# Regrouping the attention part of a decoder block: all projections of q and k first, one stretch each for turning, probabilities and values, and the unseen corners of the scores set by VectorE

## The chip, the cores and the metric

The kernel runs on one core of one Trainium2 chip. The time is device time in microseconds (us) of one execution; the reported time is the median of several runs. Engines are named TensorE (PE, and PEld for its weight loads), VectorE (DVE), ScalarE (ACT), GpSimd (POOL) and SyncE (SP, which issues the large DMAs).

## The reference

One decoder block on 256 tokens with a model width of 1024, all in float32. Two attention branches of eight heads of width 64 run side by side on the same normalised input, are gated and added; then comes a gated feed-forward part with a short convolution. With 256 tokens the block-sparse branch ("MoBA", block of 256) has a single block, so it is plain causal attention; the other branch ("FoX") adds a forgetting bias to the scores.

```python
h = rms_norm(x, attn_norm_g)
proj = h @ w_in          # qa, ka, va, qb, kb, vb (512 each), f_logit (8), g_logit (2 x 1024)
qa, ka = partial_rope(rms_norm(qa, ...)), partial_rope(rms_norm(ka, ...))
o_a = causal_softmax(qa @ ka.T / 8) @ va
qb, kb = rms_norm(qb, ...), rms_norm(kb, ...)
c = cumsum(log_sigmoid(f_logit + b_forget))
o_b = causal_softmax(qb @ kb.T / 8 + c[t] - c[s]) @ vb
gates = sigmoid(g_logit + b_gate)
merged = gates[0] * (o_a @ w_branch_moba) + gates[1] * (o_b @ w_branch_fox)
x = x + merged @ w_out
u, g = split(rms_norm(x, ffn_norm_g) @ w_ffn_up)
x = x + (silu(causal_conv3(g)) * u) @ w_ffn_down
```

## The kernel before, in words

Every large product is made from three matmuls of a shorter float32 form (`F32R`): each weight and each activation is split in a high and a low part, and high times high, high times low and low times high are added. Weights come from memory in chunks of 128 x 2048 (1 MB), in the order of the list `chunks`, by DMAs on SP's queue into three buffers (`raw`, `RB`). Each half chunk (128 x 1024) is split once: ScalarE casts it to `whi` (L136) and VectorE subtracts to get `wlo` (L137). There are six buffers of each (`HB`), and `use` asks for the split five halves ahead (`AHEAD`). A half chunk then feeds 24 matmuls of 256 columns (`twin`, L511 to L513) or 12 of 512 (`project`, L291).

TensorE's instructions run in the order in which the program writes them (`manual_schedule`). The order of the other engines is worked out by the compiler's planner, from readiness and from priorities; `soon()` raises the priority of what stands in it, and `after(i, j)` puts instruction i behind j on the same engine.

PSUM has eight banks. `bank()` takes one of them for every result that TensorE makes: a projection takes two, a gate one, the scores of a branch six, `turn` six, `turn_qk` two, the values of a branch two. A bank comes free when its readers are done.

The attention part consists of these pieces. `project_qk` projects q and k of the MoBA branch while x arrives; `project(2)` and `project(5)` make V of the two branches, `project(3)` and `project(4)` q and k of FoX. `finish_qk` normalises q or k (and turns by the rotary angles for MoBA) on ScalarE and VectorE. `turn_qk` (L341) transposes q or k by TensorE in 16 small products, and ScalarE copies the results to `qT` and `kT` (L346). `scores` (L434) multiplies q and k; because of the causal mask only some of each 128 x 128 or 128 x 256 area is computed, in pieces of 64 rows, and the corners that no product fills get something finite by small bf16 products of ones (L437). `softmax` takes the row maxima and masks by VectorE (L448), exponentials by ScalarE (L451), and scales by VectorE (L453, L456). `turn` (L467) transposes the probabilities in 48 small products per branch; ScalarE copies them out (L471). `values` (L483) multiplies them with V; ScalarE and VectorE split the result into `oh` and `ol` (L497, L498). The forgetting bias is made by `forget_a` (L362, products with the forget weights), `forget_b` (L372), `forget_chain` (small functions, a running sum by VectorE, L388, and two DMAs on POOL's queue that spread it over the partitions, L391 and L393) and `forget_bias` (five VectorE operations of 128 x 1024, L408 to L414). Eight `gate(c)` are products of two half chunks each; VectorE reads the result (L520) and the sigmoids (L524) follow later.

Before, TensorE goes through them thus: q and k of MoBA; project(2); project(3); forget_a and two turns; the first half of project(4), with forget_b within; scores(0); the rest of project(4); project(5); gate(0); two turns and turn(0); gate(1); values(0) and scores(1); gate(2) to gate(6); turn(1); gate(7); values(1); then the branch products (L609 to L611), the output product and the feed-forward part, which do not change.

Of the kernel before, what the change touches and what calls it, by code (L numbers as in the profile page):

```python
# [8 lines left out]
F32 = mybir.dt.float32  # L9
# [8 lines left out]
P = 128  # L18
# [26 lines left out]
def decoder_block(ctx, tc, a, out):  # L45
# [35 lines left out]

    chunks = [("qkv", m, h) for m in range(4) for h in range(2)]
    chunks += [("wg", c) for c in range(KT)]
    chunks += [("wb", c) for c in range(4)]
# [17 lines left out]
    def load(upto):  # L102
        while state["next"] <= min(upto, len(units) - 1):
# [30 lines left out]
            for j in range(n):  # L134
                s = slice(j * w, (j + 1) * w)
                i = nc.scalar.activation(hi[:, s], raw[:, s], AF.Copy)  # L136
                d = nc.vector.tensor_tensor(lo[:, s], raw[:, s], hi[:, s].bitcast(F32), op=ALU.subtract)  # L137
                if (c, h) == (("qkv", 0, 1), 0):
                    after(i, rs_done[0])
                    after(d, rs_done[1])  # L140
                if (c, h) == (("qkv", 0, 0), 0):
                    first_lo.append(d)
                if c[0] == "head" and j == 0:
                    after(d, xlo)
# [91 lines left out]
    def norm1_sums():  # L236
        nc.scalar.activation(flat[:, 0], xss[:, 1], AF.Copy)
        low = nc.gpsimd.tensor_tensor(flat[:, 1], xss[:, 1], flat[:, 0].bitcast(F32), op=ALU.subtract)
        for i in casts:
            after(i, low)  # L240
        ssp = bank()[:, 0:S]
        for i in range(2):
            nc.tensor.matmul(ssp, first_ones, flat[:, i], start=(i == 0), stop=(i == 1))
        return ssp
# [48 lines left out]
    def finish_v(pt, m):  # L293
        c = slice(m * W4, (m + 1) * W4)
        nc.scalar.activation(V[:, 0, c], pt[0], AF.Copy, scale=rs[:, 0:1])
        for r, q in (halves, halves[::-1]):
            nc.scalar.activation(V[r, 1, c], pt[1][q], AF.Copy, scale=rs[q, 1:2])

    def finish_qk(br, pts):
        n = len(pts)  # L300
# [10 lines left out]
        for m, (isk, pt) in enumerate(pts):  # L311
            qn = T([P, NT, NH, HD], "qn", 2)
            qns.append(qn)
            for t in range(NT):
                nc.vector.tensor_tensor(qn[:, t], pt[t].rearrange("p (h d) -> p h d", h=NH),
                                        f[:, m, t, :, None].to_broadcast([P, NH, HD]), op=ALU.mult)
            if br == 0:
                rc, rsn = rope[isk]
                p1 = T([P, NT, NH, 16], "p1", 1)
                p2 = T([P, NT, NH, 16], "p2", 1)  # L320
                x16 = qn[:, :, :, 0:16]
                nc.vector.tensor_tensor(p1, x16, rc[:, :, None, :].to_broadcast([P, NT, NH, 16]), op=ALU.mult)
                nc.vector.tensor_tensor(p2, x16, rsn[:, :, None, :].to_broadcast([P, NT, NH, 16]), op=ALU.mult)
                nc.vector.tensor_tensor(qn[:, :, :, 0:8], p1[:, :, :, 0:8], p2[:, :, :, 8:16], op=ALU.add)
                nc.vector.tensor_tensor(qn[:, :, :, 8:16], p1[:, :, :, 8:16], p2[:, :, :, 0:8], op=ALU.add)
        return qns


    qT = T16(4, "qT", F32)
    kT = T16(4, "kT", F32)  # L330
    halves = (slice(0, HD), slice(HD, P))

    def turn_qk(qn, br, isk):
# [3 lines left out]
        for t in range(NT):  # L337
            for b in range(4):
                for h, r in enumerate(halves):
                    src = qn[r, t, 2 * b:2 * b + 2].rearrange("p h d -> p (h d)")  # L340
                    nc.tensor.transpose(tp[h][:, (4 * t + b) * HD:(4 * t + b + 1) * HD], src, ident[r, r])  # L341
        dst = (kT if isk else qT).rearrange("p b (m c) -> p m b c", m=4)
        places = (slice(2, 0, -1), slice(3, None, -3)) if isk else (slice(0, 4, 2), slice(1, 4, 2))
# [22 lines left out]
    def row(i):  # L366
        return gates[:NH, i // 2, i % 2]

# [47 lines left out]

    oh = T16(KT, "oh")
    ol = T16(KT, "ol")
    probs = {}
    last_exp = []  # L420

    def scores(br):
# [5 lines left out]
        for n, pair in enumerate(range(4)):  # L428
            for t in range(NT):
                for c, q in enumerate(QUARTERS[t]):  # L430
                    seen, unseen = (slice(0, (q + 1) * HD), slice((q + 1) * HD, P)) if t == 0 else (slice((3 - q) * HD, S), slice(0, (3 - q) * HD))
                    keys = slice(seen.start + (1 - t) * P, seen.stop + (1 - t) * P)
                    for j, r in enumerate(halves):
                        nc.tensor.matmul(piece(n, t, j)[halves[c], seen], qT[r, pair, q * HD:(q + 1) * HD], kT[r, pair, keys], start=True, stop=True)  # L434
                    if q % 2 == 0:
                        for j, r in enumerate(halves):
                            nc.tensor.matmul(piece(n, t, j)[halves[c], unseen], warm[r, 0:HD], warm[r, 0:HD], start=True, stop=True)  # L437
        return [[[piece(n, t, j) for t in range(NT)] for j in range(2)] for n in range(4)]

    def softmax(br, pair, sps):  # L440
        s = T([P, 2, 384], "s", 4)
        nm = T([P, 2, 2], "nm", 4)
        l = T([P, 2, 2], "l", 4)
        for j in range(2):
            h = 2 * pair + j
            sp = sps[j]
            for i, c in enumerate((slice(0, 128), slice(128, 384))):
                nc.vector.tensor_tensor_reduce(s[:, j, c], sp[i], mask3[:, c] if br == 0 else bias[:, h, c],  # L448
                                               scale=1.0, scalar=3e38, op0=ALU.add, op1=ALU.min, accum_out=nm[:, j, i:i + 1])
            for i, c in enumerate((slice(0, 128), slice(128, 384))):  # L450
                last_exp[:] = [nc.scalar.activation(s[:, j, c], s[:, j, c], AF.Exp, scale=-1.0, bias=nm[:, j, i:i + 1], accum_out=l[:, j, i:i + 1])]  # L451
# [8 lines left out]
    def turn(br):  # L460
        pT = T([P, 4, 2, 384], "pT")
        tps = [banks() for _ in range(3)]
# [11 lines left out]

    def values(br):
        ops = banks()
        o4 = [o.rearrange("p (h b t) -> p h b t", h=2, b=4) for o in ops]

        def product(o, r, k, b, c, pair, j, start, stop):
            vc = br * W4 + (2 * pair + j) * HD  # L480
# [4 lines left out]
        one, two, both, full = slice(0, 1), slice(1, 2), slice(0, 2), slice(0, P)  # L485
        for i, k, b, c in ((0, 0, 0, two), (1, 0, 2, both), (1, 1, 1, two)):
            for pair in range(4):
                for j, m in enumerate(halves):
                    product(o4[i][m, c, pair], full, k, b, c, pair, j, b != 1 and pair == 0, False)
        for pair in range(4):  # L490
            for j, m in enumerate(halves):
                product(o4[0][m, 0, pair], halves[0], 0, 0, one, pair, j, False, pair == 3)
                product(o4[1][m, 0, pair], halves[1], 1, 1, one, pair, j, False, pair == 3)
        b = slice(4 * br, 4 * br + 4)
        for i in range(2):
            h, l = (v[:, b, i * P:(i + 1) * P].rearrange("p b (h t) -> p h b t", h=2) for v in (oh, ol))
            nc.scalar.activation(h, o4[i], AF.Copy)  # L497
            nc.vector.tensor_tensor(l, o4[i], h.bitcast(F32), op=ALU.subtract)  # L498


# [15 lines left out]

    def gate(c):
        gp = bank()
        twin("wg", c, gp, xh, xl)
        return nc.vector.tensor_tensor(gates[:, c], gp.rearrange("p (b t) -> p b t", b=2), rsB[:, None, :].to_broadcast([P, 2, S]), op=ALU.mult)  # L520
# [12 lines left out]

    pq, pk, pv = banks(), banks(), banks()
    for k in range(KT):
# [7 lines left out]
    with soon():  # L543
        qn, kn = finish_qk(0, ((0, pq), (1, pk)))
    project(2, pv, 0)
    project(2, pv, 1)
    finish_v(pv, 0)
    pq, pk = banks(), banks()
    project(3, pq, 0)
    project(3, pq, 1)  # L550
    with soon():
        forget_a()
    turn_qk(qn, 0, 0)
    turn_qk(kn, 0, 1)
    with soon():
        qn, = finish_qk(1, ((0, pq),))
    def between():
        with soon():
            forget_b()
    project(4, pk, 0, between)  # L560
    with soon():
        sps = scores(0)
        for pair in range(2):
            done = softmax(0, pair, sps[pair])
    forget_chain(done)
    project(4, pk, 1)
    with soon():
        kn, = finish_qk(1, ((1, pk),))
    for pair in range(2, 4):
        done = softmax(0, pair, sps[pair])  # L570
    pv = banks()
    project(5, pv, 0)
    project(5, pv, 1)
    finish_v(pv, 1)
    first = gate(0)
    with soon():
        forget_bias(first)
    turn_qk(qn, 1, 0)
    turn_qk(kn, 1, 1)
    turn(0)  # L580
    gate(1)
    values(0)
    for pair, sp in enumerate(scores(1)):
        softmax(1, pair, sp)
    gate(2)
    gate(3)
    gate(4)
    gate(5)
    gate(6)
    turn(1)  # L590
    gate(7)
    values(1)
    sig = [gate_sigmoid(c) for c in range(KT)]
    tables = [nc.scalar.preload_act_table_set("natural_log_exp_and_others")]
    for i in sig:
        after(tables[0], i)
# [202 lines left out]
```

## Time and profile before

| | us |
|---|---|
| runs before (3): median, lowest, highest | 362.5, 362.5, 362.65 |
| the profiled execution: its own time | 362.39 |
| the profiled execution: span from the first to the last instruction | 360.6 |

The profile is a record of one execution. Its page gives, for each engine, the time it was busy and the share of the span; the chain that ended last, followed back from the last instruction; and the costliest groups of instructions, with source line, tiles, shapes, count, busy time and the mean of one in ns. A timeline lists an engine's instructions in order of time: start, duration, engine, line, operation, output tile <- inputs, shape and count; in brackets stands how long the engine was idle before it and what ended that. Matmuls overlap, so that the distance between two starts, not the duration shown, is what one costs. A table of waits says which engine waited for what, for how long in all, how often, and how long at most. The granted clock of TensorE was 0.998 over the span.

### The profile page before, as it was taken

How to read it: one execution, taken by the hardware profiler on the slowest of the kernel's cores; microseconds unless marked ns; L12 is line 12 of the kernel's file. 1: busy time of each engine (PE TensorE's matmuls, PEld its weight loads, DVE VectorE, ACT ScalarE, POOL GpSimd, SP SyncE). 2: the span in 40 equal slices, each digit the busy share in tenths (PEclk: the TensorE clock that was granted, in tenths of full speed). 3: DMA queues.
4: the chain of work that ended last, by engine and by line, in shares of the span. 5: the costliest groups of instructions: out<-in, count | busy, mean ns of one | idle time of the engine just before them, and what ended most of it. 6: DMA issues, size and time to landing. Idle time of an engine off the chain costs nothing.

```text
span 360.6 us, 7612 instructions
## 1 busy us (share of the span) xinstructions
PE 355.4 (99%) x3151; PEld 337.5 (94%) x3151; DVE 274.3 (76%) x471; ACT 218.3 (61%) x363; POOL 28.1 (8%) x43
## 2 busy tenths in 40 slices
PE   9999999999999999999999999999999999999995
PEld 4888878899999999999999999999999999999994
DVE  4899699999887547885969776868677776768643
ACT  5859667888697774545877654655464554555420
POOL 2542002300010000000530000000000000000000
PEclk9999999999999999999999999999999999999999
DMA  7987665373606644456364564464564464563003
GB/s 275 400 318 244 238 233 183 126 257 141 234 10 235 231 170 150 159 219 201 151 223 171 193 234 162 189 234 153 199 232 164 190 234 145 205 220 132 3 0 116
DMA packets 12130, 68.28 MB, mean 189 GB/s; under 512 B 1688, under 2 KB 2848, under 8 KB 4672
## 3 DMA queue, kind: packets, MB, share of 16 engines
q1 hardware_dynamic: 11664, 66.62, 51.3%
q0 software_dynamic: 288, 1.19, 1.0%
q8 instruction: 24, 0.39, 0.4%
q14 instruction: 10, 0.08, 0.1%
q10 hardware_dynamic: 144, 0.00, 0.0%
HBM read 66.75 MB, written 1.06 MB: 188 GB/s over the span
## 4 chain that ended last, share of the span: by engine, by line
PE 99%; DVE 0%; issue 0%
PE bank L511 15%; PE bank L512 15%; PE bank L513 15%; PE bank L291 12%; PE bank L277 6%; PE bank L712 6%; PE bank L713 6%; PE bank L711 6%; PE bank L609 2%; PE bank L611 2%; PE bank L637 2%; PE bank L610 2%; PE bank L636 2%; PE bank L635 2%; PE bank L483 1%; PE bank L434 1%
## 5 line engine op out<-in xcount | busy, mean ns | idle before, releaser
L137 DVE TENSOR_TENSOR wlo<-raw,whi 128x1024 fp32r<-128x1024 f32 x120 | 147.0, 1229 | 52.6 <-ACT whi L136 52.2
L136 ACT ACTIVATE whi<-raw 128x1024 fp32r<-128x1024 f32 x120 | 126.3, 1058 | 75.5 <-PE bank L512 44.6
L513 PE MATMUL bank<-oh,wlo 128*128 128x256 f32 x352 | 96.8, 275 | 0.0
L511 PE MATMUL bank<-oh,whi 128*128 128x256 f32 x352 | 96.8, 275 | 0.0
L512 PE MATMUL bank<-ol,whi 128*128 128x256 f32 x352 | 96.8, 275 | 0.0
L511 PEld LDWEIGHTS bank<-oh,whi 128*128 128x128 f32 x352 | 66.1, 188 | 0.0
L513 PEld LDWEIGHTS bank<-oh,wlo 128*128 128x128 f32 x352 | 66.1, 188 | 0.0
L512 PEld LDWEIGHTS bank<-ol,whi 128*128 128x128 f32 x352 | 66.1, 188 | 0.0
L511 PE MATMUL bank<-xh,whi 128*128 128x256 f32 x128 | 35.6, 278 | 0.0
L513 PE MATMUL bank<-xh,wlo 128*128 128x256 f32 x128 | 35.2, 275 | 0.0
L512 PE MATMUL bank<-xl,whi 128*128 128x256 f32 x128 | 35.2, 275 | 0.0
L511 PEld LDWEIGHTS bank<-xh,whi 128*128 128x128 f32 x128 | 24.0, 188 | 0.4 <-DVE nm L448 0.2
L512 PEld LDWEIGHTS bank<-xl,whi 128*128 128x128 f32 x128 | 24.0, 188 | 0.0
L513 PEld LDWEIGHTS bank<-xh,wlo 128*128 128x128 f32 x128 | 24.0, 188 | 0.0
L291 PE MATMUL bank<-whi,xh 128*128 128x512 f32 x64 | 21.2, 392 | 0.0
L291 PE MATMUL bank<-whi,xl 128*128 128x512 f32 x64 | 21.0, 388 | 0.0
L291 PE MATMUL bank<-wlo,xh 128*128 128x512 f32 x64 | 21.0, 388 | 0.0
L678 DVE TENSOR_TENSOR sq<-bank,rs 128x512 f32<-128x512 f32 x22 | 15.1, 692 | 6.6 <-PE bank L513 6.5
L609 PE MATMUL bank<-oh,whi 128*128 128x256 f32 x64 | 17.7, 277 | 0.0
L611 PE MATMUL bank<-oh,wlo 128*128 128x256 f32 x64 | 17.6, 275 | 0.0
L610 PE MATMUL bank<-ol,whi 128*128 128x256 f32 x64 | 17.6, 275 | 0.0
L635 PE MATMUL bank<-xh,whi 128*128 128x256 f32 x64 | 17.6, 275 | 0.0
(180 smaller groups left out, 748.5 us busy)
## 6 DMA issues: line engine op xcount, KB each, us to landing
raw<-in_wu SPq DMA_DIRECT2D x22, 1024.0 KB, 4.8
raw<-in_wd SPq DMA_DIRECT2D x11, 1024.0 KB, 4.8
raw<-in_qkv SPq DMA_DIRECT2D x8, 1024.0 KB, 5.3
raw<-in_wg SPq DMA_DIRECT2D x8, 1024.0 KB, 4.8
raw<-in_wb SPq DMA_DIRECT2D x4, 1024.0 KB, 4.8
raw<-in_wo SPq DMA_DIRECT2D x4, 1024.0 KB, 4.8
raw<-in_head SPq DMA_DIRECT2D x6, 512.0 KB, 6.6
gates<-cd POOLq DMA_DIRECT2D x1, 1024.0 KB, 5.3
```

Of the source, the lines that this page charges most:

```text
L136: i = nc.scalar.activation(hi[:, s], raw[:, s], AF.Copy)
L137: d = nc.vector.tensor_tensor(lo[:, s], raw[:, s], hi[:, s].bitcast(F32), op=ALU.subtract)
L277: nc.tensor.matmul(pt[t], lhs[:, k, t * P:(t + 1) * P], rhs, start=(k == 0 and i == 0), stop=(k == KT - 1 and i == 2))
L291: nc.tensor.matmul(pt[t], lhs[:, k, t * P:(t + 1) * P], rhs[:, c], start=(k == 0 and i == 0), stop=(k == KT - 1 and i == 2))
L511: nc.tensor.matmul(o, wh[:, w], mh[:, k], start=(k == 0 and i == 0), stop=False)
L512: nc.tensor.matmul(o, wh[:, w], ml[:, k], start=False, stop=False)
L513: nc.tensor.matmul(o, wl[:, w], mh[:, k], start=False, stop=(k == KT - 1 and i == 1))
L609: nc.tensor.matmul(o, wh[:, w], oh[:, 4 * br + k], start=(k == 0), stop=False)
L610: nc.tensor.matmul(o, wh[:, w], ol[:, 4 * br + k], start=False, stop=False)
L611: nc.tensor.matmul(o, wl[:, w], oh[:, 4 * br + k], start=False, stop=(k == 3))
L635: nc.tensor.matmul(o, wh[:, w], mh[:, k], start=(k == 0 and i == 0), stop=False)
L711: nc.tensor.matmul(o, wh[:, w], ah, start=(p == 0 and h == 0 and c == 0), stop=False)
```

## The change

The order of the pieces on TensorE becomes: q and k of MoBA; project(3); project(4); gate(0); gate(1); four turns and forget_a; gate(2) with forget_b within; scores(0); project(2); gate(3); scores(1); project(5); gate(4); gate(5); turn(0) and turn(1); gate(6); values of both branches; gate(7). The list of chunks follows that order. The corners of the scores are set to zero by VectorE: ten memsets on 64 partitions for each branch, eight corners of 64 columns for each half of the heads, instead of 16 bf16 products. In each branch the first reductions of a softmax are put behind VectorE's reading of the gate before it. Because both branches are now alive together, q and k of FoX and its probabilities get homes in tiles that are free at that time (`oh`, `ol`, `qn`, `bias`), and the small rows of the forget chain move to the second half of `gates`. The sum for the first norm goes to the bank of the warm-up matmuls.

```diff
-    chunks = [("qkv", m, h) for m in range(4) for h in range(2)]
-    chunks += [("wg", c) for c in range(KT)]
+    chunks = []
+    for m in (1, 2, "wg0", "wg1", "wg2", 0, "wg3", 3, "wg4", "wg5", "wg6", "wg7"):
+        chunks += [("wg", int(m[2:]))] if isinstance(m, str) else [("qkv", m, h) for h in range(2)]
...
-        ssp = bank()[:, 0:S]
+        ssp = wp[:, 0:S]
...
     def row(i):
-        return gates[:NH, i // 2, i % 2]
+        return gates[:NH, 4 + i // 2, i % 2]
...
                     for j, r in enumerate(halves):
-                        nc.tensor.matmul(piece(n, t, j)[halves[c], seen], qT[r, pair, q * HD:(q + 1) * HD], kT[r, pair, keys], start=True, stop=True)
-                    if q % 2 == 0:
-                        for j, r in enumerate(halves):
-                            nc.tensor.matmul(piece(n, t, j)[halves[c], unseen], warm[r, 0:HD], warm[r, 0:HD], start=True, stop=True)
+                        nc.tensor.matmul(piece(n, t, j)[halves[c], seen], qTs[br][r, pair, q * HD:(q + 1) * HD], kTs[br][r, pair, keys], start=True, stop=True)
+        for b, c, o in ((0, 0, slice(64, 512, 384)), (0, 1, slice(128, 129, 1)), (1, 1, slice(0, 512, 256)), (2, 0, slice(64, 256, 128)), (2, 1, slice(256, 257, 1))):
+            for j in range(2):
+                starts = range(o.start, o.stop, o.step)
+                u = sps[b][j][halves[c]].rearrange("p (g c) -> p g c", c=HD)[:, o.start // HD:starts[-1] // HD + 1:max(1, o.step // HD)]
+                nc.vector.memset(u, 0.0)
...
-    def softmax(br, pair, sps):
+    def softmax(br, pair, sps, done):
...
-                nc.vector.tensor_tensor_reduce(s[:, j, c], sp[i], mask3[:, c] if br == 0 else bias[:, h, c],
+                first = nc.vector.tensor_tensor_reduce(s[:, j, c], sp[i], mask3[:, c] if br == 0 else bias[:, h, c],
                                                scale=1.0, scalar=3e38, op0=ALU.add, op1=ALU.min, accum_out=nm[:, j, i:i + 1])
+                after(first, done)
...
+    for isk in range(2):
+        pt = banks()
+        project(3 + isk, pt, 0)
+        project(3 + isk, pt, 1)
+        with soon():
+            qkn += finish_qk(1, ((isk, pt),))
+    gate(0)
+    gate(1)
+    for i, qn in enumerate(qkn):
+        turn_qk(qn, i // 2, i % 2)
+    with soon():
+        forget_a()
...
+    read = gate(2, between)
+    with soon():
+        for pair, sp in enumerate(scores(0)):
+            scaled = softmax(0, pair, sp, read)
+            if pair == 1:
+                done = scaled
+    forget_chain(done)
+    pv = banks()
     project(2, pv, 0)
     project(2, pv, 1)
     finish_v(pv, 0)
+    read = gate(3)
     with soon():
+        forget_bias(read)
     with soon():
+        for pair, sp in enumerate(scores(1)):
+            softmax(1, pair, sp, read)
     pv = banks()
     project(5, pv, 0)
     project(5, pv, 1)
     finish_v(pv, 1)
     gate(4)
     gate(5)
+    turn(0)
+    turn(1)
     gate(6)
+    oh, ol, copied = values()
     gate(7)
```

In the new `values()` all products over whole rows of both branches come first, then those over half rows, branch by branch, each followed by its copies to `oh` and `ol`.

More of the change, by code (lines that the diff above doesn't have):

```diff
@@ L137, in load @@
                 d = nc.vector.tensor_tensor(lo[:, s], raw[:, s], hi[:, s].bitcast(F32), op=ALU.subtract)
-                if (c, h) == (("qkv", 0, 1), 0):
+                if (c, h) == (("qkv", 1, 1), 0):
                     after(i, rs_done[0])
                     after(d, rs_done[1])
-                if (c, h) == (("qkv", 0, 0), 0):
+                if (c, h) == (("qkv", 1, 0), 0):
                     first_lo.append(d)
@@ L297, in finish_v @@
             nc.scalar.activation(V[r, 1, c], pt[1][q], AF.Copy, scale=rs[q, 1:2])
+    qn1 = T16(KT, "ol", F32)
     def finish_qk(br, pts):
@@ L311, in finish_qk @@
         for m, (isk, pt) in enumerate(pts):
-            qn = T([P, NT, NH, HD], "qn", 2)
+            if br == 0:
+                qn = T([P, NT, NH, HD], "qn", 2)
+            else:
+                qn = qn1[:, 4 * isk:4 * isk + 4].rearrange("p k t -> p (k t)").rearrange("p (t h d) -> p t h d", t=NT, h=NH)
             qns.append(qn)
@@ L326, in finish_qk @@
         return qns
-    qT = T16(4, "qT", F32)
-    kT = T16(4, "kT", F32)
+    qk1 = T16(KT, "oh", F32)
+    qTs = T16(4, "qT", F32), qk1[:, 0:4]
+    kTs = T16(4, "kT", F32), qk1[:, 4:8]
     halves = (slice(0, HD), slice(HD, P))
@@ L341, in turn_qk @@
                     nc.tensor.transpose(tp[h][:, (4 * t + b) * HD:(4 * t + b + 1) * HD], src, ident[r, r])
-        dst = (kT if isk else qT).rearrange("p b (m c) -> p m b c", m=4)
+        dst = (kTs if isk else qTs)[br].rearrange("p b (m c) -> p m b c", m=4)
         places = (slice(2, 0, -1), slice(3, None, -3)) if isk else (slice(0, 4, 2), slice(1, 4, 2))
@@ L414, in forget_bias @@
                 nc.vector.tensor_tensor(dst, dst, mask3[:, None, j * P:(j + 1) * P].to_broadcast([P, NH, P]), op=ALU.add)
-    oh = T16(KT, "oh")
-    ol = T16(KT, "ol")
     probs = {}
+    homes = []
     last_exp = []
@@ L430, in scores @@
                 for c, q in enumerate(QUARTERS[t]):
-                    seen, unseen = (slice(0, (q + 1) * HD), slice((q + 1) * HD, P)) if t == 0 else (slice((3 - q) * HD, S), slice(0, (3 - q) * HD))
+                    seen = slice(0, (q + 1) * HD) if t == 0 else slice((3 - q) * HD, S)
                     keys = slice(seen.start + (1 - t) * P, seen.stop + (1 - t) * P)
                     for j, r in enumerate(halves):
-                        nc.tensor.matmul(piece(n, t, j)[halves[c], seen], qT[r, pair, q * HD:(q + 1) * HD], kT[r, pair, keys], start=True, stop=True)
-                    if q % 2 == 0:
-                        for j, r in enumerate(halves):
-                            nc.tensor.matmul(piece(n, t, j)[halves[c], unseen], warm[r, 0:HD], warm[r, 0:HD], start=True, stop=True)
-        return [[[piece(n, t, j) for t in range(NT)] for j in range(2)] for n in range(4)]
-    def softmax(br, pair, sps):
-        s = T([P, 2, 384], "s", 4)
+                        nc.tensor.matmul(piece(n, t, j)[halves[c], seen], qTs[br][r, pair, q * HD:(q + 1) * HD], kTs[br][r, pair, keys], start=True, stop=True)
[4 more added lines that the diff above has]
+                nc.vector.memset(u, 0.0)
+        return [[[piece(n, t, j) for t in range(NT)] for j in range(2)] for n in range(4)]
+    def softmax(br, pair, sps, done):
+        if br == 0:
+            s = T([P, 2, 384], "s", 4)
+        else:
+            if not homes:
+                two = T([P, KT * S + 64], "ol")
+                homes.extend(two[:, i * 768:(i + 1) * 768] for i in range(2))
+                homes.extend(T([P, 1024], "qn", 2)[:, 0:768] for i in range(2))
+            s = homes[pair].rearrange("p (j c) -> p j c", j=2)
         nm = T([P, 2, 2], "nm", 4)
@@ L460, in turn @@
     def turn(br):
-        pT = T([P, 4, 2, 384], "pT")
+        pT = T([P, 4, 2, 384], ("pT", "bias")[br])
         tps = [banks() for _ in range(3)]
@@ L473, in turn, with values, product @@
             probs[br, pair] = pT[:, pair]
[L475 to L479, printed above, removed]
+    def values():
+        oh, ol = T16(KT, "oh"), T16(KT, "ol")
+        ops = [banks() for br in range(2)]
+        o4s = [[o.rearrange("p (h b t) -> p h b t", h=2, b=4) for o in ops[br]] for br in range(2)]
+        def product(o, r, k, b, c, br, pair, j, start, stop):
             vc = br * W4 + (2 * pair + j) * HD
@@ L485, in values @@
         one, two, both, full = slice(0, 1), slice(1, 2), slice(0, 2), slice(0, P)
-        for i, k, b, c in ((0, 0, 0, two), (1, 0, 2, both), (1, 1, 1, two)):
+        for br, o4 in enumerate(o4s):
+            for i, k, b, c in ((0, 0, 0, two), (1, 0, 2, both), (1, 1, 1, two)):
+                for pair in range(4):
+                    for j, m in enumerate(halves):
+                        product(o4[i][m, c, pair], full, k, b, c, br, pair, j, b != 1 and pair == 0, False)
+        for br, o4 in enumerate(o4s):
             for pair in range(4):
                 for j, m in enumerate(halves):
[L489 to L498, printed above, removed]
+                    product(o4[0][m, 0, pair], halves[0], 0, 0, one, br, pair, j, False, pair == 3)
+                    product(o4[1][m, 0, pair], halves[1], 1, 1, one, br, pair, j, False, pair == 3)
+            b = slice(4 * br, 4 * br + 4)
+            for i in range(2):
+                h, l = (v[:, b, i * P:(i + 1) * P].rearrange("p b (h t) -> p h b t", h=2) for v in (oh, ol))
+                copied = nc.scalar.activation(h, o4[i], AF.Copy)
+                nc.vector.tensor_tensor(l, o4[i], h.bitcast(F32), op=ALU.subtract)
+        return oh, ol, copied
     def twin(kind, c, dst, mh, ml, late=False, between=None):
@@ L515, in twin, with gate @@
                     between()
-    def gate(c):
+    def gate(c, between=None):
         gp = bank()
-        twin("wg", c, gp, xh, xl)
+        twin("wg", c, gp, xh, xl, between=between)
         return nc.vector.tensor_tensor(gates[:, c], gp.rearrange("p (b t) -> p b t", b=2), rsB[:, None, :].to_broadcast([P, 2, S]), op=ALU.mult)
@@ L532, in banks @@
         return [bank() for _ in range(NT)]
-    pq, pk, pv = banks(), banks(), banks()
+    pq, pk = banks(), banks()
     for k in range(KT):
@@ L543, in decoder_block, with between @@
     with soon():
-        qn, kn = finish_qk(0, ((0, pq), (1, pk)))
+        qkn = finish_qk(0, ((0, pq), (1, pk)))
+    for isk in range(2):
[10 more added lines that the diff above has]
+        forget_a()
+    def between():
+        with soon():
+            forget_b()
+    read = gate(2, between)
+    with soon():
+        for pair, sp in enumerate(scores(0)):
[4 more added lines that the diff above has]
+    pv = banks()
     project(2, pv, 0)
@@ L547, in decoder_block @@
     finish_v(pv, 0)
-    pq, pk = banks(), banks()
-    project(3, pq, 0)
-    project(3, pq, 1)
+    read = gate(3)
     with soon():
-        forget_a()
-    turn_qk(qn, 0, 0)
-    turn_qk(kn, 0, 1)
+        forget_bias(read)
     with soon():
[L556 to L570, printed above, removed]
+        for pair, sp in enumerate(scores(1)):
+            softmax(1, pair, sp, read)
     pv = banks()
@@ L574, in decoder_block @@
     finish_v(pv, 1)
[L575 to L586, printed above, removed]
     gate(4)
     gate(5)
+    turn(0)
+    turn(1)
     gate(6)
-    turn(1)
+    oh, ol, copied = values()
     gate(7)
-    values(1)
     sig = [gate_sigmoid(c) for c in range(KT)]
     tables = [nc.scalar.preload_act_table_set("natural_log_exp_and_others")]
-    for i in sig:
+    for i in sig + [copied]:
         after(tables[0], i)
```

## The prediction

> **What bounds the kernel now.** I read the busy line and the chain of the page first, then TensorE's and its weight load's waits, then TensorE's timeline around each place where the change moves something, and then VectorE's and ScalarE's timelines there.
>
> ```profile
> span 360.6 us, 7612 instructions
> PE 355.4 (99%) x3151; PEld 337.5 (94%) x3151; DVE 274.3 (76%) x471; ACT 218.3 (61%) x363; POOL 28.1 (8%) x43
> PE 99%; DVE 0%; issue 0%
> PEld bank L277 <- DVE wlo L137: 0.9, 3, 0.3
> ```
>
> The chain of waits lies on TensorE for 99%, and the weight loads waited 0.9 us for the splits, all of it in the start (L277). So the change can gain only what shortens TensorE's own stream, and it loses whatever makes TensorE wait. About 0.2% (0.7 us) is what can be told from no change here.
>
> The stream of weight matmuls keeps a fixed step, 0.113 us for 256 columns (122.35 to 122.46 below), so 24 of them, a half chunk, take 2.72 us. It is broken by six stretches of small matmuls: forget_a with two turns; scores(0); two turns with turn(0); values(0) with scores(1); turn(1); values(1). One of them, turn(1), and the two switches inside stretches:
>
> ```profile
> 122.35 0.28 PE L512 MATMUL bank<-xl,whi 128*128 128x256 f32 x1
> 122.46 0.28 PE L513 MATMUL bank<-xh,wlo 128*128 128x256 f32 x1
> 122.67 1.72 PE L467 MATMUL bank<-cst,s 64*128 64x64 f32 x48
> 124.31 0.39 PE L511 MATMUL bank<-xh,whi 128*128 128x256 f32 x1
> 124.54 0.28 PE L512 MATMUL bank<-xl,whi 128*128 128x256 f32 x1
> ...
> 131.63 0.34 PE L483 MATMUL bank<-pT,V 128*64 128x64 f32 x6
> 131.96 0.29 PE L483 MATMUL bank<-pT,V 64*64 64x64 f32 x4
> ...
> 49.06 1.07 PE L362 MATMUL bank<-xT,wfg 128*32 128x256 f32 x16
> 50.07 1.21 PE L341 MATMUL bank<-cst,qn 64*128 64x64 f32 x32
> 51.20 0.49 PE L291 MATMUL bank<-whi,xh 128*128 128x512 f32 x1
> ```
>
> The first stream matmul that turn(1) displaces was due at 122.57 and, counted back from 124.54, the stream is in step again from 124.43: 1.86 us. Its 24 pairs step by 0.061 us (1.46 us), so entering, draining and leaving cost 0.40 us a stretch. A switch of tile inside costs less: at 131.96 the next pair was due at about 131.86, and it restarts slowly, some 0.15 us in all.
>
> **The change part by part.**
>
> *One stretch fewer.* After: four turns with forget_a; scores(0); scores(1); turn(0) with turn(1); both values. Five for six: -0.40 us. Inside, values changes from whole to half rows once instead of twice, and turns and forget_a still meet once: two switches for three, -0.15 us. Projections and gates change places; each half is 2.72 us wherever it stands, and the chunks' list moves in step, each load the same 1024 KB on SP's queue, so nothing there.
>
> *Corners.* Each scores call makes 16 bf16 products of 64 columns (L437) that the memsets replace.
>
> ```profile
> 57.73 0.20 PE L437 MATMUL bank<-const-bfloat16-1.0 64*64 64x64 bf16 x2
> 57.76 0.30 PE L434 MATMUL bank<-kT,qT 64*64 64x128 f32 x6
> 57.88 0.20 PE L437 MATMUL bank<-const-bfloat16-1.0 64*64 64x64 bf16 x2
> 58.33 0.20 PE L437 MATMUL bank<-const-bfloat16-1.0 64*64 64x64 bf16 x2
> ```
>
> A pair of heads takes 0.60 us (57.73 to 58.33). On each half of the columns one corner sits in the row of products: 57.73 to 57.76 is 0.03 us, the lower bound. The other corner (57.88) stands in the way of the products issued behind it and can cost as much again, since all start in order. I take 0.055 us a pair, eight pairs: -0.44 us (bounds -0.22 to -0.50).
>
> *The wait in the turns.* All work shares eight PSUM banks; turns fill them and ScalarE empties them.
>
> ```profile
> 82.70 1.92 PE L467 MATMUL bank<-cst,s 64*128 64x64 f32 x48
> 83.91 0.71 PE L467 MATMUL bank<-cst,s 64*128 64x64 f32 x15
> 84.55 0.39 PE L511 MATMUL bank<-xh,whi 128*128 128x256 f32 x1
> 81.64 1.06 ACT L136 ACTIVATE whi<-raw 128x1024 fp32r<-128x1024 f32 x1 [1.66 <-PE bank L512]
> 82.61 1.25 ACT L346 ACTIVATE qT<-bank,gq 128x512 f32<-128x512 f32 x2
> 84.89 3.05 ACT L471 ACTIVATE pT<-bank 128x512 f32<-128x512 f32 x6
> 123.69 0.49 ACT L524 ACTIVATE gates<-gates,sm 128x256 f32<-128x256 f32 x1
> 124.08 3.01 ACT L471 ACTIVATE pT<-bank 128x512 f32<-128x512 f32 x6
> ```
>
> The stretch from 81.65 needs ten banks; the last two are waited for until ScalarE, busy with a cast until 82.61, has emptied two, at 83.86: turn(0) goes on at 83.91, and turn(0) here takes 1.85 us where turn(1) took 1.64. That wait goes: -0.19 us. But turn(0) with turn(1) needs twelve banks. From its start at T, a group of 16 transposes takes 0.49 us; the fifth group (T+2.0) needs two banks empty, the sixth (T+2.5) four. ScalarE takes the cast of the half whose buffer has just come free, T to T+1.0, then 0.50 us a bank (3.05 us for six): two at T+2.0, four at T+3.0. So the sixth waits: +0.49 us. If ScalarE begins at once there is no wait; with a gate's sigmoid between cast and copies, as at 123.69, it is 0.9. In the first stretch four turns fill exactly eight banks, gate(1)'s being read 0.7 us after T and needed at T+1.6; forget_a's is the first emptied: 0.
>
> *VectorE.* Its work is hidden as long as the splits stay ahead of TensorE.
>
> ```profile
> 81.76 0.69 DVE L520 TENSOR_TENSOR gates<-bank,rsB 128x512 f32<-128x512 f32 x1 [0.51 <-PE bank L513]
> 82.37 1.22 DVE L411 TENSOR_TENSOR bias<-gates,cc 128x1024 f32<-128x1024 f32 x1
> 88.04 2.35 DVE L137 TENSOR_TENSOR wlo<-raw,whi 128x1024 fp32r<-128x1024 f32 x2
> 94.78 0.28 DVE L448 CUSTOM_DVE_ANT_0 s<-bank,bias 128x128 f32<-128x128 f32 x1
> 97.00 0.18 DVE L453 RECIPROCAL r<-l 128x4 f32<-128x4 f32 x1 [0.27 <-ACT s L451]
> 101.91 1.22 DVE L137 TENSOR_TENSOR wlo<-raw,whi 128x1024 fp32r<-128x1024 f32 x1
> L456 DVE TENSOR_SCALAR s<-s,r 128x128 f32<-128x128 f32 x16 | 4.5, 281 | 0.0
> L448 DVE DVE_READ_ACCUMULATOR2_ANT nm<- 128x1 f32 x32 | 2.6, 83 | 0.0
> ```
>
> The 20 memsets (64 partitions, 64 or 128 elements) have no row. Between the smallest VectorE instruction (0.08 us) and a 128x128 one (0.28) I take 0.19: 1.9 us a branch (0.8 to 2.8). They stand ahead of the softmax, and all reductions behind them wait. The Trainium skill (VectorE: DVE Perf Modes, Zero memsets can be issued as uint32) gives a memset one cycle per element; with the 0.96 GHz of Trainium Kernel Development and Optimization (NeuronCore Architecture) that is an estimated 1.1 us a branch for its 1024 elements, without a fixed cost, and the count of the next paragraph would then end 0.8 us earlier, on time; no run so far shows a memset in PSUM.
>
> The tight place is after gate(3). Before, bias (82.37 to 88.04, 5.67 us) and softmax(1) (94.78) lay apart, with splits and 8 us of small matmuls between. Now they adjoin. Counting from the end of gate(3): evacuation until 0.7, bias until 6.4, memsets until 8.3, softmax(1) until its first split (7.13 us by 94.78 to 101.91) 15.4, that split 16.6. TensorE, with six buffers (HB), wants that half (gate(4)'s second, whose buffer came free at 0) after scores(1) (four pairs of 0.55 us and 0.40: 2.6) and five halves: 16.2. So in strict order it is 0.4 us late, and 1.6 us if one more split was owed when bias began. But its cast is done at 1.1, so it can go into any idle moment of VectorE, of the kind that stands before 97.00. The trace cannot tell: in that softmax no split was ready earlier. I take 0, bounds 0 and 2.5 (one split owed, memsets at 0.28). Elsewhere there is cover: softmax(0) after scores(0) has 16.3 us (six halves) until scores(1) wants its banks; the two later finish_qk stand 10.9 us apart and their results are wanted only at the turns.
>
> *The forget chain* starts later too.
>
> ```profile
> 60.02 0.28 DVE L448 CUSTOM_DVE_ANT_0 s<-bank,cst 128x128 f32<-128x128 f32 x1
> 68.76 0.58 POOL L393 DMA_DIRECT2D gates<-cd  x1
> gates<-cd POOLq DMA_DIRECT2D x1, 1024.0 KB, 5.3
> ```
>
> Its scan waits for the second pair's softmax, and the last of its DMAs is issued 8.7 us behind softmax(0)'s first reduction and lands 5.3 us later. After the end of gate(2) come scores(0) and the memsets (4 us), so it lands at 18; bias wants it after scores(0), project(2), gate(3) and an evacuation: 2.6 + 10.9 + 5.4 + 0.7 = 19.6. Hidden by 1.6 us; if late, VectorE stops in front of bias with splits queued behind it.
>
> *Rows, homes, banks, sigmoids.* Other buffers, the same instructions. values(1) stands a gate earlier than before, so its copies get 5.4 us more cover. 0.
>
> **Sum.** -0.40 -0.15 -0.44 -0.19 +0.49 = -0.69 us. The profiled execution took 362.39 us, 1.79 around its span of 360.6, which the change doesn't touch: 361.7. The median of the runs is 0.11 above it: 361.8.
>
> **The rivals.**
>
> *No wait in the turns.* ScalarE empties from T+0.6 on: against it, at 81.64 and at each gate's end it takes the cast. Then 361.8 - 0.5 = 361.3.
>
> *VectorE late after gate(3).* For it, the count above with no slack; against it, the ready split needs only one gap. 1.6 us: 363.4; it ends slower once it is over 1.4 us (from -0.69 to +0.7), and at its bound 2.5 us it is 364.3.
>
> *The change does little.* Corners at their lower bound (+0.22) and turns at 0.9 (+0.4): 362.4, no change.
>
> *The clock falls.* In the long transpose stretch the grant could drop, and the first half chunk behind it would take double: +2.72, 364.5. Against it, the clock stands at 1.00 through the transposes of before:
>
> ```profile
> 81.60:84.60 3.00, 3.00 (x83) 2.77 (x81) 2.84 (x3) 2.96 (x5) 0.00 (x0) 1.00 0.87 347
> ```
>
> The Trainium skill (TensorE: Matmul & The Clock Gate, Part 4) says that transposes don't count as work for the gate in the same way, and Part 1 puts the window at 3.4 us; the new stretch takes 3.8 us by the rows above (48 pairs of 0.061, 0.40 and 0.49). The trace shows no drop in 2.9 us, and no run before has more.
>
> **How the numbers follow.** Forecast 46% (361.4 to 362.2; 0.28 of it below 361.78, the 0.2% line, 0.18 above); no wait in the turns 12%, faster; little 11%, same; VectorE late 24% (0.11 same, 0.13 slower); clock 3% and a wait in the new order that I don't foresee 4%, slower. Faster 0.40, same 0.40, slower 0.20. The range reaches from 361.1 (0.2 us below the rival without a wait, since the price of a stretch is read off one of six) to 363.5 (VectorE late by 1.6 us), leaving out the rest.
>
> **What would show it.** Right: TensorE with five stretches, no L437 row, scores stretches shorter by about 0.2 us each, a gap of half a microsecond within L467's last group that ends when ScalarE has emptied the fourth bank, TensorE's sum of waits else unchanged. Wrong: TensorE or its weight loads waiting for wlo about 16 us after gate(3), or for banks in gate(4); or VectorE idle before bias, waiting for the DMA of cB; or a granted clock below 1.00 behind the turns.

## The result, and the profile after

| | us |
|---|---|
| before, 4 runs beside it | 362.57 (362.5 to 362.71) |
| after, 4 runs | 367.82 (367.15 to 368.02) |
| ratio, 95% interval | 1.0144 (1.0132 to 1.0156) |
| the profiled execution of after: own time, span | 367.73, 365.9 |

The changed kernel is 5.25 us slower. The forecast was 361.8 with a range to 363.5, so it failed in sign and in size. Times and ratios here leave out two disturbed executions, one of a1 (600.65 us, the only one of a1 with a trace) and one of a3 (727.45 us).

The first lines of the page of after, its busy line and its chain of waits:

```profile
span 365.9 us, 7562 instructions
PE 357.4 (98%) x3119; PEld 340.3 (93%) x3119; DVE 275.8 (75%) x491; ACT 218.1 (60%) x363; POOL 26.8 (7%) x43
PE 84%; ACT 7%; DVE 6%; issue 1%; ACTq 0%
```

Before, the chain lay on TensorE for 99%. Now 13% of it runs over ScalarE and VectorE: TensorE stood still somewhere for work of theirs. The table of waits between 110 and 123 us (engine, line, what it waited for, total us, times, longest) says where:

```profile
PEld bank L483 <- DVE gates L539: 3.0, 2, 2.7
PE bank L483 <- DVE gates L539: 2.6, 1, 2.6
PEld bank L483 <- ACT pT L487: 1.0, 3, 0.3
```

L483 is the transposing of the probabilities. It waited for banks: first for VectorE's reading of two gates (L539), then for ScalarE's copies (L487). No row names wlo, the wait that the prediction feared. TensorE's timeline there (start, duration, engine, line):

```profile
112.85 1.72 PE L483 MATMUL bank<-cst,s 64*128 64x64 f32 x48
114.70 0.27 PE L483 MATMUL bank<-cst,ol 64*128 64x64 f32 x1
118.89 0.46 PE L483 MATMUL bank<-cst,ol 64*128 64x64 f32 x7 [0.21 <-ACT pT L487]
119.13 1.84 PE L483 MATMUL bank<-cst,qn 64*128 64x64 f32 x24
...
120.90 0.58 PE L530 MATMUL bank<-xh,whi 128*128 128x256 f32 x1
121.28 0.41 PE L531 MATMUL bank<-xl,whi 128*128 128x256 f32 x1
```

turn(0) runs through in 1.5 us. turn(1) (tiles `ol` and `qn`) gets its first bank at 114.70, and its next product starts 2.87 us later. Between starts there are then 0.37, 0.48 and 0.48 us more, each ended by a copy. The stretch lasts 112.85 to 120.90, 8.05 us; without a wait it is 3.3 (d1 below: 3.51 with one wait of 0.25). Behind it the stream steps by 0.213 us instead of 0.113: the clock. Windows of the span (PE busy, PEld, DVE, ACT, POOL, granted clock, DMA share, GB/s):

```profile
112.60:116.00 3.40, 2.24 (x52) 1.84 (x51) 3.40 (x6) 3.39 (x5) 0.00 (x0) 1.00 0.84 296
116.00:119.40 3.40, 1.49 (x32) 1.22 (x32) 2.73 (x3) 3.40 (x8) 0.00 (x0) 1.00 0.76 263
119.50:122.80 3.30, 3.15 (x28) 2.85 (x26) 0.00 (x0) 3.30 (x8) 0.00 (x0) 0.50 0.86 308
122.90:126.20 3.30, 3.30 (x31) 3.30 (x30) 0.00 (x0) 3.30 (x9) 0.00 (x0) 1.00 0.12 50
```

For 3.41 us (119.44 to 122.85) the granted clock is half. It slows the last transposes, and the 48 matmuls behind take 6.59 us instead of 5.69 (a3 below). Two of the four runs of after show a granted clock of 0.991 over the span where the profiled one shows 0.994. One such stretch at half costs 3.41 x 0.5 of 366 us, 0.005, so I estimate that they had about two.

Why the banks were not free: VectorE's timeline from the end of gate(3), which TensorE left at 88.4.

```profile
88.80 1.22 DVE L138 TENSOR_TENSOR wlo<-raw,whi 128x1024 fp32r<-128x1024 f32 x1 [0.34 <-ACT whi L137]
89.94 0.68 DVE L539 TENSOR_TENSOR gates<-bank,rsB 128x512 f32<-128x512 f32 x1
90.54 1.21 DVE L418 TENSOR_TENSOR bias<-gates,cc 128x1024 f32<-128x1024 f32 x1
...
96.39 1.52 DVE L445 MEMSET bank<- 64x128 f32 x10
97.82 0.27 DVE L463 CUSTOM_DVE_ANT_0 ol<-bank,bias 128x128 f32<-128x128 f32 x1
...
111.90 1.00 DVE L472 TENSOR_SCALAR qn<-qn,r 128x128 f32<-128x128 f32 x4
112.82 1.22 DVE L138 TENSOR_TENSOR wlo<-raw,whi 128x1024 fp32r<-128x1024 f32 x1
113.96 0.68 DVE L539 TENSOR_TENSOR gates<-bank,rsB 128x512 f32<-128x512 f32 x1
114.56 2.35 DVE L138 TENSOR_TENSOR wlo<-raw,whi 128x1024 fp32r<-128x1024 f32 x2
116.83 0.68 DVE L539 TENSOR_TENSOR gates<-bank,rsB 128x512 f32<-128x512 f32 x1
```

Bias, memsets and softmax(1), with five splits among them, last until 112.8. The readings of gate(4) (done on TensorE 5.4 us before the turns) and of gate(5) (done as the turns begin) come at 113.96 and 116.83, behind splits that nobody was waiting for. Until then two of the eight banks are held; six are turn(0)'s. ScalarE's timeline shows why those were not free either:

```profile
110.57 2.00 ACT L137 ACTIVATE whi<-raw 128x1024 fp32r<-128x1024 f32 x2
112.58 1.28 ACT L543 ACT_TABLE_LOAD   x1
113.88 0.51 ACT L543 ACTIVATE gates<-gates,sm 128x256 f32<-128x256 f32 x1
114.29 1.04 ACT L137 ACTIVATE whi<-raw 128x1024 fp32r<-128x1024 f32 x1
115.24 1.69 ACT L543 ACTIVATE gates<-gates,sm 128x256 f32<-128x256 f32 x4
116.83 1.04 ACT L137 ACTIVATE whi<-raw 128x1024 fp32r<-128x1024 f32 x1
117.78 3.00 ACT L487 ACTIVATE pT<-bank 128x512 f32<-128x512 f32 x6
```

The first copy starts 4.9 us after the stretch began, behind a table load (1.28 us), five sigmoids and two casts.

**Where the 5.34 us between the two profiled executions are** (starts of matmuls compared): the turns with their waits and slow transposes, 8.05 instead of 3.3, +4.8; the stream behind at half clock, +0.9; the first sum of norm 1 is multiplied at 24.68 instead of 24.23, +0.45 (the clock rose at 6.8 instead of 4.1 us; the traces of after and its variants below, whose start is the same, have it between 3.8 and 6.8); at the very end +0.1. The rest, which was forecast as a gain, came to about -0.9.

### The profile page after: what moved, and what is told of

The parts are those of the page before. It is cut to its first block, busy times and chain, and to the rows that moved or that the text cites. A ratio compares the mean times of both kernels' runs of the same rounds, so it can differ in the third digit from the quotient of the medians.

```text
span 365.9 us, 7562 instructions
## 1 busy us (share of the span) xinstructions
PE 357.4 (98%) x3119; PEld 340.3 (93%) x3119; DVE 275.8 (75%) x491; ACT 218.1 (60%) x363; POOL 26.8 (7%) x43
## 3 DMA queue, kind: packets, MB, share of 16 engines
q0 software_dynamic: 288, 1.19, 1.0%
## 4 chain that ended last, share of the span: by engine, by line
PE 84%; ACT 7%; DVE 6%; issue 1%; ACTq 0%
PE bank L530 13%; PE bank L532 13%; PE bank L531 13%; PE bank L278 6%; PE bank L292 6%; PE bank L729 5%; PE bank L727 5%; PE bank L728 5%; ACT whi L137 3%; PE bank L651 2%; PE bank L625 2%; PE bank L653 2%; PE bank L652 2%; PE bank L627 2%; PE bank L626 2%; DVE wlo L138 2%
```

## The experiments

My theory (A): TensorE stands still because both kinds of bank are held, the gates' by VectorE and turn(0)'s by ScalarE; the stop then lowers the clock. The rivals: one of the two engines alone is the cause, VectorE above all; and the transposes themselves lower the clock. The expectations say what each would give.

### a1: the sigmoids behind the turns

```diff
-            after(i, last_exp[0])
+            after(i, last_copy[0])      # gate_sigmoid; last_copy: the last copy of turn(1)
```

> The changed kernel, but ScalarE's gate sigmoids stand behind the last copy of the turned probabilities; VectorE's order is untouched. Theory A (in the changed kernel TensorE stops in the turns because two of the eight banks still hold gates 4 and 5, which VectorE reads late, and because ScalarE starts its copies late; each of the two alone is enough to hold TensorE): the stop of 2.9 us that ends with VectorE's read of gate(5) stays, the three later waits for copies (0.3, 0.4 and 0.4 us) shrink, 366.5 to 367.2. Theory B (the stretch of transposes by itself lowers the clock and that is most of the loss): 367.8, as the changed kernel. Theory C (ScalarE's late copies alone are the cause): 363 or less.

Measured: 366.13 (365.81 to 367.12, three runs), ratio 1.0109 (1.0089 to 1.0129). With ScalarE free early 1.7 us come back, which puts the time 0.4 us below theory A's range, and 3.7 us of loss remain: ScalarE alone isn't the cause. That the stop for VectorE's reading stays is argued here from the time, since there is no trace to show it; the granted clocks of its three runs, 0.991 to 0.995 against 0.998 to 1.0 in the runs of the kernel before, say that the clock still fell.

### a2: the gates read at once

VectorE reads gates 4 and 5 as soon as they are done; the splits that stood ahead wait (`use` asks for 2 and 4 halves fewer there, and the next splits stand behind the reading of gate(5)).

```diff
-        load(... pos[c, h] + AHEAD)
+        load(... pos[c, h] + AHEAD - {("wg", 4): 2, ("wg", 5): 4}.get(c, 0))
...
+                if held: after(d, held[0])          # d: the split
...
-    gate(5)
+    held[:] = [gate(5)]
...
-        return nc.vector.tensor_tensor(gates[:, c], gp...
+        with tc.high_priority(offset=120 if c in (4, 5) else 0): return nc.vector.tensor_tensor(gates[:, c], gp...
```

> The changed kernel, but VectorE reads gates 4 and 5 ahead of the last probabilities' scaling and of the splits of later weights; ScalarE's order of sigmoids and copies is untouched. Theory A: the stop moves to the fifth group of transposes, which waits for ScalarE's copies; little is won, 366.3 to 367.8. If VectorE's late reads alone are the cause: 363 or less. Theory B: 367.8.

Measured: 367.85 (367.62 to 368.05), ratio 1.015 (1.0135 to 1.0165): nothing gained. Its waits between 108 and 122 us:

```profile
PE bank L484 <- ACT pT L488: 3.3, 1, 3.3
```

And ScalarE's timeline:

```profile
112.01 1.28 ACT L544 ACT_TABLE_LOAD   x1
...
117.21 3.00 ACT L488 ACTIVATE pT<-bank 128x512 f32<-128x512 f32 x6
```

TensorE waits for VectorE no more. It now stops for 3.56 us between two starts, ended by ScalarE's first copy, which starts at 117.21, 4.9 us into the stretch as in after; the stretch again takes 8.05 us. VectorE alone isn't the cause either.

### a3: both

> Both edits of the two kernels before together. Theory A: TensorE's stretch of turns falls from 8.1 us to about 3.5 us, the clock stays at 1.00 behind it, 362.0 to 362.8, which is what is left of the change. Theory B: the stretch is shorter but the clock still falls to half behind it for some 3 us, 363.5 or more.

Measured: 362.52 (362.11 to 363.02), ratio 1.0004 (0.9994 to 1.0014). Two edits that gave 1.7 and 0.0 us alone give 5.3 together. The waits of the turns:

```profile
PEld bank L484 <- ACT pT L488: 0.7, 2, 0.3
```

And ScalarE's timeline:

```profile
109.72 3.89 ACT L137 ACTIVATE whi<-raw 128x1024 fp32r<-128x1024 f32 x4
113.51 3.00 ACT L488 ACTIVATE pT<-bank 128x512 f32<-128x512 f32 x6
```

The stretch takes 4.21 us, where I expected about 3.5; two starts come 0.48 us behind the one before, since ScalarE casts until 1.5 us into it. The clock stays at 1.00. Either hold is enough to stop TensorE, and the half clock went with the stop. VectorE has as much to do here as in after.

### b1: the corners alone, in the kernel before

The bf16 products are replaced by the memsets and nothing else.

> The kernel before with one part of the change alone: the corners of the scores by VectorE's memsets. By the prediction TensorE's two stretches of scores get 0.22 us shorter each (0.11 to 0.25): 362.1 (361.9 to 362.4); a memset takes 0.19 us (0.08 to 0.28) on VectorE. If VectorE's added work is what makes the changed kernel late, TensorE waits here too and the time is above 362.5.

Measured: 362.05 (361.59 to 362.18), ratio 0.9987 (0.9978 to 0.9997), -0.39 us. scores(0) takes 2.34 us instead of 2.56.

### c1: a3 with every transpose of the turns done twice

> The kernel a3 (sigmoids behind the last turn copy, gates 4 and 5 read at once) with every transpose of the probabilities done twice into the same place; the output does not change. This asks whether transposes by themselves lower the clock, or the stop. In a3 the stretch took 4.21 us, two waits of 0.48 among it, at clock 1.00. Done twice, 96 pairs at 0.061 us and 0.40 for going in and out make 6.3 us; the banks fill at half the rate, so the two waits for the copies should be gone. Theory A (a stop of about 3 us among the transposes lowers the clock): no drop, stretch 6.1 to 6.5 us, time 362.5 + 2.1 = 364.6 (364.2 to 365.0). Theory B (a stretch of transposes longer than the 3.41 us of one clock record lowers it, stop or not): at least one stretch of 3.41 us at half clock, transposes at 0.10 to 0.12 us a pair and the stream behind slower by about 1 us: 365.5 to 368.

Measured: 364.71 (364.14 to 364.77). The stretch takes 6.15 us. Two windows inside it:

```profile
112.70:115.70 3.00, 3.00 (x97) 3.00 (x98) 2.92 (x4) 3.00 (x6) 0.00 (x0) 1.00 0.15 22
115.70:118.80 3.10, 3.10 (x103) 3.06 (x99) 3.10 (x4) 3.10 (x8) 0.00 (x0) 1.00 0.92 325
```

192 transposes and nothing else for 6.15 us, 3.0 and 3.1 us of two clock records of 3.41, at clock 1.00 there and behind: theory B of this run falls. The Trainium skill (TensorE: Matmul & The Clock Gate, Part 4) says that the transpose mode doesn't count as busy for the gate in the same way. For the transposes of this kernel the clock of 1.00 doesn't bear that out, and the measurement decides; whether they run in the mode that the page means, the trace doesn't tell.

### c2 and c4: the turns apart

```diff
     gate(4)
-    gate(5)
     turn(0)
+    gate(5)
     turn(1)
     gate(6)
```

> The changed kernel with turn(0) between gate(4) and gate(5), and turn(1) between gate(5) and gate(6); nothing else changes, VectorE reads the gates as late as before and the sigmoids stay free. If the cause is that twelve banks are wanted within one stretch while six are in copying and two are unread, then 5.4 us of gate(5) between the two lets ScalarE copy turn(0)'s six banks out (3.0 us), and no late read matters. Theory A: the stop of 2.87 and the three waits of 0.37, 0.48 and 0.48 go, the clock stays at 1.00, one stretch more costs 0.40: from a3, which had two waits of 0.48 left, 362.5 - 0.96 + 0.40 = 362.0 (361.6 to 362.6). Theory C (VectorE's lateness itself is the cost, through splits or anything else it owes by then): it stops TensorE wherever it owes the read of gate(4) or a split, and 365 or more remains.

> As c2 (turns apart), and the sigmoids behind the last turn copy, so that ScalarE copies each bank as soon as it can. Theory A: c2's ScalarE has the copies of turn(0) ahead of the sigmoids already, so this changes c2 by nothing on TensorE, unless turn(1)'s banks are still waited for in c2: 361.6 to 362.4, within 0.5 us of c2. If ScalarE's sigmoids, now all behind the turns, come too late for the branch products' gating, it is slower than c2 by a wait behind values.

Measured: c2 362.79 (362.3 to 363.29), ratio 1.0009 (1.0 to 1.0019); c4 362.73 (362.36 to 363.11), 1.0008 (0.9999 to 1.0018). In c2 VectorE reads gate(4) as late as in after, at 113.39 (second row below, of VectorE's timeline), and TensorE doesn't stop for it. One edit to the order does what two edits to VectorE and ScalarE do in a3, and theory C of that run falls. That brings the time back to that of the kernel before, and no lower. The two are 0.2 and 0.3 us above the ranges of A; c2's waits show why:

```profile
PE bank L483 <- ACT V L298: 0.5, 1, 0.5
...
113.39 0.68 DVE L539 TENSOR_TENSOR gates<-bank,rsB 128x512 f32<-128x512 f32 x1
```

Moved up by 5.4 us, turn(0) meets the banks of project(5), which ScalarE is still emptying: one start comes 0.73 us behind the one before. turn(1) runs clean in 1.64 us, as before the change. c4 is the same within 0.1 us: the sigmoids don't matter once the turns are apart.

### a5: the corners by TensorE again, the rest as after

> The changed kernel with the corners of the scores made by TensorE again, as before, so VectorE has 1.5 us less to do between gate(3) and the turns. Scores cost 0.44 us more. Theory A: the read of gate(5) comes 1.5 us earlier and the stop shortens from 2.87 to about 1.4 us, if ScalarE's copies come earlier by as much (they stand behind sigmoids that wait for the last exponential, which is earlier too): 367.8 + 0.45 - 1.5 = 366.8 (366.0 to 367.3), or 365.9 if the clock then stays at 1.00. If the memsets are nothing to the stop, 368.3.

Measured: 368.86 (368.46 to 369.51), ratio 1.0179 (1.0163 to 1.0196): slower by 1.0, where I expected a gain of 1.0. Its waits:

```profile
PE bank L481 <- DVE gates L537: 1.9, 1, 1.9
PE bank L481 <- ACT pT L485: 0.9, 1, 0.9
```

And ScalarE's timeline:

```profile
114.38 2.09 ACT L541 ACTIVATE gates<-gates,sm 128x256 f32<-128x256 f32 x5
116.37 1.04 ACT L137 ACTIVATE whi<-raw 128x1024 fp32r<-128x1024 f32 x1
117.32 1.06 ACT L485 ACTIVATE pT<-bank 128x512 f32<-128x512 f32 x2
```

VectorE is earlier and the stop for it shorter (gaps between starts of 2.13 instead of 2.87), but ScalarE takes seven sigmoids first and starts copying at 117.32, so the next gap is 1.08 instead of 0.37. The gaps add up to 4.2 us in both. The half clock lasts 6.83 us here instead of 3.41. Without the memsets the change is as slow: they alone are not what made it so.

### d1: a3 with the copies first

```diff
-                if held: after(d, held[0])
+                if held: after(d, held[0]), (c, h) in ((("wg", 7), 1), (("wb", 0), 0)) and after(i, first_copies[-1])
```

Here `d` is the split, `i` the cast, and `first_copies` holds the copies of turn(0); the line ahead is a3's.

> The kernel a3 (sigmoids behind the last turn copy, gates 4 and 5 read at once), and the casts of the second half of gate(7) and of the first half behind it stand behind the copies of turn(0), so that ScalarE begins to copy when the first banks are full (half a microsecond into the stretch) and not 1.5 us into it. That is the case without a wait in the turns which the prediction gave 361.3. Theory A: the two waits of 0.48 in a3 go, the stretch falls from 4.21 to 3.3 us, 362.5 - 0.96 = 361.6 (361.2 to 361.9), 0.2 to 0.3% below the kernel before; TensorE then asks for the held splits 6 us and more behind the turns. If the two waits in a3 were not for the late copies: 362.5. If the held casts come too late for TensorE: a wait for wlo in gate(7) or in the branch products, and 362 or more.

Measured: 361.97 (361.5 to 362.32), ratio 0.9985 (0.9976 to 0.9994). ScalarE's timeline:

```profile
110.57 1.05 ACT L137 ACTIVATE whi<-raw 128x1024 fp32r<-128x1024 f32 x1
113.61 3.04 ACT L488 ACTIVATE pT<-bank 128x512 f32<-128x512 f32 x6 [1.99 <-PE bank L484]
116.48 1.11 ACT L137 ACTIVATE whi<-raw 128x1024 fp32r<-128x1024 f32 x1
```

Now ScalarE waits for the banks, not TensorE for ScalarE; copies start 0.75 us into the stretch. The stretch takes 3.51 us, with one start 0.25 us late. That is 0.7 us better than a3 in the trace where I expected 0.96, and 0.55 in the time; the median lies 0.07 above the expected range. It is faster than both kernels, by 5.9 and 0.44 us, but not clearly by more than b1 (0.39), which only replaces the corners.

### d3: a stop without transposes around it

> The kernel a3 with a stop of TensorE put where there are no transposes around it: behind the second pair of branch products one small transpose waits for VectorE's product of that pair and four sums of 128x256 by GpSimd (about 0.8 us each by a3's rows), so TensorE stands 4 to 5.5 us with plain matmuls of 256 columns before and behind. The added sums are used by nothing. It asks whether standing still is enough to lower the clock. Theory A (idle time of about 2 us and more within one clock record of 3.41 us, whatever is around it): the record behind the stop is at half, matmuls there step by 0.213 instead of 0.113 us, and the time is 362.5 + stop + 0.9 to 1.7. Theory B' (the stop lowers it only together with transposes): clock 1.00 throughout, 362.5 + stop.

Measured: 368.15 (368.11 to 368.19). TensorE's timeline at the end of the stop:

```profile
147.72 0.27 PE L638 MATMUL bank<-cst,p 64*128 64x64 f32 x1 [4.15 <-POOL p L637]
```

And the windows around it:

```profile
144.90:148.30 3.40, 0.58 (x4) 0.52 (x5) 3.38 (x4) 0.83 (x2) 2.60 (x3) 1.00 0.20 58
148.40:151.70 3.30, 3.30 (x18) 3.30 (x17) 0.00 (x0) 0.00 (x0) 0.00 (x0) 0.50 0.75 308
151.80:155.10 3.30, 3.30 (x31) 3.30 (x30) 1.49 (x2) 1.06 (x1) 0.00 (x0) 1.00 0.00 0
```

The gap of 4.43 us costs 5.63: standing still lowers the clock with plain matmuls on both sides. Neither side of it had transposes, and c1 had transposes without a stop.

## Why the prediction was wrong

**The step that failed is the wait in the turns.** It said: "From its start at T, a group of 16 transposes takes 0.49 us; the fifth group (T+2.0) needs two banks empty". That takes all eight banks as free at T. Two of them belonged to gate(4) and gate(5), and I didn't ask when VectorE reads those, though I had asked it for gate(1) in the first stretch, and though the next part of the prediction counted VectorE until 16.6 us after gate(3), while gate(4) ends 18.9 us after it and gate(5) at T. The second half of the step put ScalarE's copies at T+1.0, with 0.9 us of wait as the worst, from a single sigmoid between cast and copies. The trace showed T+4.9: the sigmoids become free with the last exponential, which now ends some 2 us before T, and the planner put their table load and five of them ahead of the copies. Forecast +0.49 (0 to 0.9); found +4.8 with the slow transposes. Each of the two assumptions, alone, is enough for the stop: a2's trace shows it for ScalarE's late copies; for VectorE's late readings it follows from the stop that they end in after and from the time of a1.

**VectorE after gate(3)** was the right place and the wrong victim. The rival said that TensorE would wait for wlo. Its count began late: in after a split stood before the reading of gate(3), which ended 2.2 us after the gate instead of 0.7, so bias ended at 7.9 instead of 6.4. But five splits found a place during softmax(1), though not only in "any idle moment of VectorE" (the one at 98.58 us stands between two reductions with no idle time around it), and TensorE never waited for one. What was late were the readings of the gates, behind those splits. The lateness fell on the work that had no priority, and that work held banks.

**The clock** was a rival with 3% and the wrong condition: "in the long transpose stretch". c1 and d3 show that it is the standing still. Its price, a whole half chunk doubled (+2.72), was too high: half clock for one record of 3.41 us in the profiled run, +0.9 on the stream and about 0.5 on the transposes.

**What held.** The corners: scores stretches of 2.34 us, 0.22 shorter, and -0.39 us in b1 against the forecast -0.44. The memsets: 0.15 us each, 1.5 a branch, inside the bounds 0.8 to 2.8 and below the 1.9 taken. No wait for the forget chain. No wait in the first stretch, where four turns fill all banks (3.32 us). The row of scores(0) in after, with no L437 in it:

```profile
69.66 2.41 PE L440 MATMUL bank<-kT,qT 64*64 64x64 f32 x64
```

**A smaller miss.** Without any wait the sum was -1.18 (-0.40 -0.15 -0.44 -0.19). d1, less its wait of 0.25, gives -0.94: small stretches 16.36 us instead of 16.82, and one restart of the stream fewer, -0.23. The corners (-0.45; b1's small stretches also add up to 16.36) and the old bank wait (-0.19) account for -0.64 of it, so one stretch and one switch fewer are worth about 0.3 us and not 0.55.

## What to carry to other kernels

Before you pack two stretches of small matmuls together, list who holds each PSUM bank at that moment and when its reader, in that reader's own queue, gets to it; a reading that nobody waits for today is what a late engine puts off. When two holds end together, removing one of them shows nothing (a2) or a third of the loss (a1), so try both before you drop the theory. Where such a stop is met, moving one stretch behind other work (c2, one line) can be cheaper than hurrying two engines; here either way only undoes the loss.

## What the runs showed of the hardware

TensorE's clock is granted in records of 3.41 us and falls to half for one or two of them: in every trace read here the times at which it changes lie whole multiples of 3.413 us apart (in after 6.80, 119.44, 122.85 and 365.20), which places the records between. Waiting time of TensorE inside a record (gaps over 0.3 us between starts, less 0.1) and the clock of the record behind it:

| run | record (us) | waiting | its clock | clock behind |
|---|---|---|---|---|
| c1 | 115.72 to 119.13 | 0 | 1.0 | 1.0 |
| a3 | 113.75 to 117.16 | 0.76 | 1.0 | 1.0 |
| after | 112.61 to 116.03 | 1.48 | 1.0 | 1.0 |
| d3 | 141.48 to 144.90 | 1.51 | 1.0 | 1.0 |
| a2 | 113.02 to 116.44 | 2.06 | 1.0 | 0.5 |
| after | 116.03 to 119.44 | 2.18 | 1.0 | 0.5 |
| a5 | 114.15 to 117.56 | 2.62 | 1.0 | 0.5 |
| d3 | 144.90 to 148.31 | 2.82 | 1.0 | 0.5 |
| after | 119.44 to 122.85 | 0.66 | 0.5 | 1.0 |
| a5 | 117.56 to 120.98 | 1.19 | 0.5 | 0.5 |
| a2 | 116.44 to 119.85 | 1.78 | 0.5 | 0.5 |

Here 1.5 us of 3.41 did no harm and 2.06 did; what lies between wasn't measured. A stop of 2.9 us need not fill a record to cost the clock. By this table it should also depend on where the stop falls between two records, but no run here shows a stop of that length that went free. The program doesn't choose the place: the first rise, from which the records count, came at 3.8 to 6.8 us in the traces of after and its variants. The Trainium skill (TensorE: Matmul & The Clock Gate, Part 1) gives a free-running window of 3413 ns; the trace agrees with the length. The Trainium skill says there too that the clock falls after at least one idle window; the records above with 2.06 to 2.82 us of waiting don't bear out that the window has to be wholly idle.
